# A two-layer hybrid decoder trunk on one core: all weights as one stream that the products feed, and the first block's order

## The chip, the core and the metric

The kernel runs on one core of a Trainium2 chip. The metric is the time of one execution on the device in microseconds (us). Engines are called as the profile calls them: PE is TensorE's matmul and PEld its weight load, DVE is VectorE, ACT is ScalarE, POOL is GpSimd, and SP is the engine whose queue issues nearly all of the DMAs. Every engine takes its own instructions strictly in the order of its list and waits on semaphores for what others produce.

## The reference

The input is one sequence of 512 tokens by 1024 columns in float32; the depth is two layers. Four groups of mixers share one input projection and one output projection, and the residual stream ends in an RMSNorm:

```python
h = x
for l in range(DEPTH):                       # 2 layers
    u = rmsnorm(h, norm_w[l])
    proj = einsum('bsd,de->bse', u, w_in[l])
    ret_p, diff_p, ssd_p, ml_p = split_cols(proj, ...)
    ret_out = retention_mixer(...) * silu(rz)
    diff_out = diff_attention_mixer(...) * silu(dz)
    y = ssd_mixer(...)
    ssd_out = _rms(y * silu(sz)) * ssd_norm_w[l]
    ml_out = mlstm_mixer(...) * silu(mz)
    mix = concatenate([ret_out, diff_out, ssd_out, ml_out])
    h = h + einsum('bse,ed->bsd', mix, w_out[l])
return rmsnorm(h, final_norm_w)
```

The projections are nearly all of the arithmetic. The differential attention takes two softmaxes per head over 512 tokens, and the state-space mixer ("ssd") runs four chunks of 128 tokens with a state carried between them.

## The kernel before

**Arithmetic.** A product in float32 is made of three cheaper ones. An operand x is cut into a high part hi (x rounded by a cast to the type fp32r) and a low part lo = x - hi, and a product is hi·hi + hi·lo + lo·hi, three matmuls that add up in one PSUM bank. For the activations the parts are `uh` and `ul` (lines 347, 348) or `mh` and `ml`, for the weights `whi` and `wlo`.

**Weights.** The input projection has 15 blocks of 512 columns in each layer, the output projection four groups of two halves. A block (or a group) is eight pieces of 128 x 512. `split_w` (lines 364 to 367) brings two pieces with one DMA of 512 KB into a buffer `raw`, of which there are two, and calls `split_half` (lines 351 to 362) for each: ACT writes `whi` (line 357, or 360 where a norm weight is multiplied in), DVE subtracts and writes `wlo` (358 or 361). There are ten buffers each of `whi` and `wlo`, eight in use and two ahead; the cast into a buffer waits until PE has done the last product with the piece that was there. Before the change a block's four DMAs and eight splits are all written where the block's first product is asked for (`load_block`, line 369, called from `proj_tok` and `proj_feat`, and the same in `out_proj`, lines 626 to 635), and the splits stand in a context of priority 100, which makes a scheduler draw them ahead of other work that is written near them.

**Order of the work.** PE's list is a sequence of projections, in the order of `ORDER`: mv, mq, mk, mo, mz, dk, dq, dv, dz, out_proj m, xs, bc, out_proj d, rqk, sz, rv, rz, out_proj s and r. Between the steps of a projection a planner (`drive`, `due`) inserts the steps of the mixers (gates, mlstm, diff, ssd, ret) by an own clock and by the delays in the table `W`. What goes to DVE, ACT, POOL and SP is written in the same pass, and a scheduler orders it by program order and priorities. Buffers and PSUM banks rotate: eight banks, taken from the one that comes free first.

**The first block** (projection mv of layer 0, `start`, lines 373 to 481) is the exception: its order on all engines is written by hand. Token group t (128 tokens, four of them) has squares(t) on ACT, scale(t) (an rsqrt on POOL, line 240), mul(t) (two multiplies on DVE, line 404, tiles `e`), trans(t) (eight transposes on PE, line 131, into two banks, followed by `uh` on ACT and `ul` on DVE); hi(k) and lo(k) split weight piece k. In the strings `orders`, "h3" is the two products with the high part of piece 3 and "l3" the one with its low part. At the very start `warm(4)` and `warm(3)` are matmuls of a tile of ones whose result nobody reads.

**Three other places** that the text below speaks of.

- The differential attention of a head ends with `diff_av` (lines 1148 to 1164): the weights `w` of one token group are transposed into a PSUM bank (line 131) and copied back to SBUF, on DVE for even token groups (line 1157) and on ACT for odd (1155). The bank is then given to the next product that asks for one. On DVE the copy stands in one list with the splits, the sums of the row maxima (1133), the softmax arithmetic (1138 to 1141), `diff_fin` (1177 to 1186) and the gate product `z` (544).
- A chunk of the ssd mixer has a chain on DVE: additions from a broadcast tile `bcm` (line 950), an exponential on ACT and a multiply by a PSUM tile (954), before PE can make the chunk's output (`psacc`, the matmuls that read `w`). The rotary embeddings of the rqk product come in between (`ft`, lines 604 and 606).
- The gates of the mlstm and ssd mixers (`gates`, lines 674 to 802): a scan of small DVE instructions ends in a row that goes to DRAM (`gdr`, line 779) and comes back broadcast to all partitions (`bcm`, line 813).

Of the kernel before, what the change touches and what calls it, by code (L numbers as in the profile page):

```python
# [11 lines left out]
F32 = mybir.dt.float32  # L12
# [11 lines left out]
DEPTH = 2  # L24
# [40 lines left out]
     'm0': 6.4, 's0': 8.8, 'dT1': 0.6, 'dN1': 1.0, 'hp': 100, 'he': 100, 'hr': 50, 'hd': 50, 'dS': 4.7, 'dQ': 6.0,  # L65
# [34 lines left out]
class Trunk:  # L100
    def __init__(self, ctx, tc, aps, dbg=None):
        self.tc, self.nc = tc, tc.nc
        self.x, self.win, self.wg, self.wout, self.nrm, self.rows, self.convp, self.cst, self.out = aps
        self.dbg = dbg or {}
        mk = lambda n, b, **k: ctx.enter_context(tc.tile_pool(name=n, bufs=b, **k))
        self.cp = mk("cp", 1)


        self.small = mk("small", 1)
        self.hp = mk("hp", 1)  # L110
        self.pool = mk("pool", 1)
        self.end = mk("end", 1)
        self.ps = mk("ps", 1, space=bass.MemoryType.PSUM)
        self.banks = [(0.0, b) for b in range(8)]
# [84 lines left out]
    def setup(self):  # L199
# [29 lines left out]
        warm(3)  # L229
# [121 lines left out]
    def split_half(self, raw, scale):  # L351
        nc = self.nc
        hi = self.t("whi", [P, 512], F32R, bufs=10)
        lo = self.t("wlo", [P, 512], F32R, bufs=10)
        with self.tc.high_priority(W["hp"]):
            if scale is None:
                nc.scalar.copy(out=hi, in_=raw)  # L357
                nc.vector.tensor_tensor(out=lo, in0=raw, in1=hi.bitcast(F32), op=ALU.subtract)  # L358
            else:
                nc.scalar.activation(hi, raw, AF.Copy, scale=scale)  # L360
                nc.vector.scalar_tensor_tensor(lo, raw, scale, hi.bitcast(F32), ALU.mult, ALU.subtract)  # L361
        return hi, lo
# [6 lines left out]
    def load_block(self, name):  # L369
        b = BIDX[name]  # L370
        return [q for g in range(4) for q in self.split_w(self.win[self.l, b, :, 2 * g:2 * g + 2, :])]

    def start(self, evac):
# [46 lines left out]
        with self.tc.manual_schedule(engines={E.Activation, E.DVE, E.Pool, E.SP}):  # L420
# [13 lines left out]
            orders = ["h0 h1 l0 l1 h2 h3 h4 h6 l2 h5 l4 l3 h7 l6 l5 l7", "h0 h1 h2 h3 l0 l1 l2 l3 h4 h5 h6 h7 l4 l5 l6 l7"]  # L434
# [16 lines left out]
            lo(4, nc.gpsimd)  # L451
# [4 lines left out]
            mul(1)  # L456
            lo(6, nc.gpsimd)
            lo(3)
            run(pr[0], 6)
            trans(1)  # L460
            lo(5)
            lo(7, nc.gpsimd)
            run(pr[0], 2)
# [12 lines left out]
            self.gates_w()  # L476
            run(pr[2], 8)
# [20 lines left out]
    def proj_tok(self, name, evac, w=None, toks=range(NT), order=None):  # L498
        w = w or self.load_block(name)
        steps = [(t, k, parts) for t in toks for k, parts in order] if order else \  # L500
                [(t, k, (0, 1)) for t, k in self.steps_of(list(toks), name != "mv")]
        banks, n = {}, {}
        for t, k, parts in steps:
# [6 lines left out]
            for part in parts:  # L510
                for u in (self.uh,) if part else (self.uh, self.ul):
                    n[t] += 1
                    self.mm(p, lhsT=u[:, k, ts_], rhs=w[k][part], start=(n[t] == 1), stop=(n[t] == 3 * KD))
# [6 lines left out]
    def proj_feat(self, name, evac):  # L520
        w = self.load_block(name)
        banks = {}
        for f, k in self.steps_of(range(4), True):
            p = banks[f] if k else banks.setdefault(f, self.psum("pj"))
            fs = slice(f * P, (f + 1) * P)
            hi, lo = w[k][0][:, fs], w[k][1][:, fs]
# [100 lines left out]
    def out_proj(self, g, mixt, tok_outer=False, after=None, cut=False, heads=False):  # L627
        nc = self.nc
        gi = GROUPS[g]
        nw = self.nwc[g]  # L630
        w = [[x for q in range(2) for x in self.split_w(self.wout[self.l, gi, half, :, 2 * q:2 * q + 2, :],
                                                        nw[2 * q:2 * q + 2])]
             for half in range(2)]
# [3 lines left out]
        for t, hf in order:  # L637
# [5 lines left out]
            for c0, c1 in zip(cuts, cuts[1:]):  # L643
# [5 lines left out]
                for k in range(4):  # L649
                    hi, lo = w[hf][k]  # L650
# [3 lines left out]
                    self.mm(p, lhsT=mh, rhs=lo[:, cs], start=False, stop=(k == 3))  # L654
                    yield
# [700 lines left out]
```

## Time and profile before

| what | before |
|---|---|
| median of 3 runs | 1045.69 us (1043.56 to 1046.55) |
| profiled execution, its own time | 1043.91 us |
| span from the first to the last instruction | 1042.1 us |
| PE busy | 1023.0 us, 98% of the span |
| DVE busy | 693.2 us, 67% |
| ACT busy | 479.7 us, 46% |
| POOL busy | 164.9 us, 16% |
| mean granted clock of PE | 0.994 of full speed |
| moved by DMA | 93.84 MB |

Times in rows of the profile are us from the start of the span; 1.8 us of the execution's time lie outside it. A row of the timeline gives the start, the time until the end of the group, the engine, the line, the operation and its tiles, and in brackets the idle time before it with what ended it. Matmuls overlap: a row's mean duration is longer than the distance from one to the next. A line of the kernel is written L127; L127 and L131 are the helpers through which every matmul and every transpose goes.

### The profile page before, as it was taken

The numbers are of one execution on the slowest core, as the hardware profiler recorded it, in microseconds if no ns is written. First come the engines' busy times: TensorE is split into PE (matmuls) and PEld (weight loads), VectorE is DVE, ScalarE is ACT, GpSimd is POOL, SyncE is SP. The second block draws the span as 40 slices with busy tenths as digits, with TensorE's granted clock in tenths as the row PEclk, the third lists the DMA queues.
The fourth block names the chain that finished last, engine by engine and source line by source line (L and its number), as shares of the span: only waits on it lengthen the run. The fifth ranks groups of instructions, "written<-read, shape, count | busy, mean of one in ns | idle before, by whom it ended". The sixth has DMA issues, their size and how long they took to land.

```text
span 1042.1 us, 14190 instructions
## 1 busy us (share of the span) xinstructions
PE 1023.0 (98%) x5110; PEld 835.1 (80%) x5110; DVE 693.2 (67%) x1495; ACT 479.7 (46%) x1057; POOL 164.9 (16%) x204
## 2 busy tenths in 40 slices
PE   8999999999999999999999999999999999999997
PEld 6788888877778887878887888887777888878786
DVE  5588675567787867446655967666667786863454
ACT  4444336545455444433343542575444553553332
POOL 2000132101111233022000012210001112510301
PEclk9999999999999999999999999999999999999999
DMA  7324322322212413313122422233121233233112
GB/s 254 107 72 122 102 71 82 101 82 81 79 44 85 128 51 102 102 61 126 41 84 80 138 85 81 82 101 103 60 86 56 81 100 103 81 102 101 42 60 81
DMA packets 39144, 93.84 MB, mean 90 GB/s; under 512 B 3849, under 2 KB 16777, under 8 KB 38946
## 3 DMA queue, kind: packets, MB, share of 16 engines
q1 hardware_dynamic: 38064, 91.49, 28.7%
q10 hardware_dynamic: 1010, 1.45, 0.4%
q8 instruction: 40, 0.66, 0.3%
q14 instruction: 30, 0.25, 0.1%
HBM read 90.78 MB, written 2.15 MB: 89 GB/s over the span
## 4 chain that ended last, share of the span: by engine, by line
PE 90%; DVE 5%; issue 1%; ACT 1%; DMA 1%; POOL 0%; POOLq 0%; DVEq 0%; ACTq 0%
PE pspj L127 74%; PE psS L127 6%; PE psacc L127 6%; PE psS L131 4%; DMA raw<-in_w_in_dram 1%; DVE wlo L361 1%; DVE w L950 1%; DVE ft L606 0%; DVE z L1291 0%; DVE wlo L358 0%; DVE h L657 0%; DVE z L544 0%; ACT e L253 0%; DMA raw<-in_w_out_dram 0%; DVE wlo L418 0%
## 5 line engine op out<-in xcount | busy, mean ns | idle before, releaser
L358 DVE TENSOR_TENSOR wlo<-raw,whi 128x512 fp32r<-128x512 f32 x248 | 174.0, 721 | 67.4 <-ACT whi L357 61.8
L127 PE MATMUL pspj<-whi,uh 128*128 128x512 f32 x512 | 209.7, 410 | 0.0
L127 PE MATMUL pspj<-whi,ul 128*128 128x512 f32 x512 | 200.9, 392 | 0.0
L127 PE MATMUL pspj<-wlo,uh 128*128 128x512 f32 x512 | 197.7, 393 | 2.4 <-DVE wlo L418 2.2
L357 ACT CAST whi<-raw 128x512 fp32r<-128x512 f32 x248 | 147.8, 618 | 108.5 <-PE pspj L127 60.8
L127 PE MATMUL pspj<-uh,whi 128*128 128x512 f32 x448 | 179.2, 400 | 0.0
L127 PE MATMUL pspj<-uh,wlo 128*128 128x512 f32 x448 | 174.7, 390 | 0.0
L127 PE MATMUL pspj<-ul,whi 128*128 128x512 f32 x448 | 174.6, 390 | 0.0
L127 PEld LDWEIGHTS pspj<-wlo,uh 128*128 128x128 f32 x512 | 96.5, 189 | 25.1 <-DVE wlo L418 3.9
L127 PEld LDWEIGHTS pspj<-whi,uh 128*128 128x128 f32 x512 | 97.0, 189 | 22.4 <-issue 3.0
L127 PEld LDWEIGHTS pspj<-whi,ul 128*128 128x128 f32 x512 | 96.9, 189 | 17.8 <-DVE ul L348 0.4
L127 PE MATMUL pspj<-whi,mh 128*128 128x512 f32 (+1 forms) x260 | 105.2, 405 | 4.3 <-DVE w L1157 4.3
L240 POOL TENSOR_TENSOR s<-s,nhalf 128x4 f32<-128x4 f32 (+1 forms) x44 | 35.8, 813 | 417.5 <-DVE s L1181 122.9
L127 PE MATMUL pspj<-whi,ml 128*128 128x512 f32 (+1 forms) x260 | 101.4, 390 | 0.3
L127 PE MATMUL pspj<-wlo,mh 128*128 128x512 f32 (+1 forms) x260 | 101.2, 389 | 0.0
L127 PEld LDWEIGHTS pspj<-uh,wlo 128*128 128x128 f32 x448 | 84.1, 188 | 18.2
L127 PEld LDWEIGHTS pspj<-uh,whi 128*128 128x128 f32 x448 | 84.2, 188 | 17.4 <-issue 0.7
L127 PEld LDWEIGHTS pspj<-ul,whi 128*128 128x128 f32 x448 | 84.3, 188 | 16.0
L584 DVE SCALAR_TENSOR_TENSOR e<-pspj,cvh,e 128x511 f32<-128x511 f32 (+2 forms) x90 | 67.0, 744 | 9.6 <-ACT e L582 8.4
L602 ACT ACTIVATE e<-pspj 32x512 f32<-32x512 f32 x96 | 56.6, 589 | 20.0 <-PE pspj L127 18.7
L657 DVE TENSOR_TENSOR h<-pspj,h 128x512 f32<-128x512 f32 (+1 forms) x65 | 43.6, 678 | 28.7 <-PE pspj L127 28.3
L127 PEld LDWEIGHTS pspj<-whi,mh 128*128 128x128 f32 x260 | 49.3, 190 | 15.4 <-DVE w L1157 5.2
(221 smaller groups left out, 1406.4 us busy)
## 6 DMA issues: line engine op xcount, KB each, us to landing
raw<-in_w_in_dram SPq DMA_DIRECT2D x116, 512.0 KB, 3.9
raw<-in_w_out_dram SPq DMA_DIRECT2D x32, 512.0 KB, 3.5
bcm<-adr SPq DMA_DIRECT2D x16, 256.0 KB, 3.3
z<-in_w_in_dram SPq DMA_DIRECT2D x8, 256.0 KB, 6.6
bcm<-gdr SPq DMA_DIRECT2D x8, 256.0 KB, 3.8
out_dram<-z SPq DMA_DIRECT2D x7, 256.0 KB, 2.0
h<-in_x_dram SPq DMA_DIRECT2D x3, 512.0 KB, 6.5
cst<-in_consts_dram SPq DMA_DIRECT2D x1, 1035.0 KB
```

What stands on the lines that cost most here:

```text
L127: self.nc.tensor.matmul(out, lhsT=lhsT, rhs=rhs, start=start, stop=stop, **kw)
L131: self.nc.tensor.transpose(out, src, self.ident if ident is None else ident)
L240: self.nc.gpsimd.tensor_tensor(out=out, in0=m, in1=self.nhalf[:, :n], op=ALU.pow)
L357: nc.scalar.copy(out=hi, in_=raw)
L358: nc.vector.tensor_tensor(out=lo, in0=raw, in1=hi.bitcast(F32), op=ALU.subtract)
L361: nc.vector.scalar_tensor_tensor(lo, raw, scale, hi.bitcast(F32), ALU.mult, ALU.subtract)
L584: nc.vector.scalar_tensor_tensor(acc[:, s:], p[:, 0:S - s], w[:, 3 - s:4 - s], acc[:, s:], ALU.mult, ALU.add)
L602: nc.scalar.activation(x[q * 32:q * 32 + 32, :], p[o * 32:o * 32 + 32, :], AF.Copy, scale=scale)
L657: nc.vector.tensor_tensor(out=hs, in0=p, in1=hs, op=ALU.add)
L950: nc.vector.scalar_tensor_tensor(e[:, j * P:(j + 1) * P], ab[g][:, j, :], self.ncs[:, t, h:h + 1], self.cap, ALU.add, ALU.min)
```

## The change

**One stream.** A generator `stream` walks through both layers in `ORDER` and yields two pieces at a time, with their DMA and their splits. `feed` draws one such pair from it. `piece(key, k)` returns a piece and feeds until it is there. `proj_tok`, `proj_feat` and `out_proj` take their pieces with `piece` and call `feed` right after the last product with a pair of pieces (the last token or feature group, odd k). So a pair's DMA and splits are now written at the place in the program at which two buffers come free, over the whole kernel, and in particular the first pieces of a block are written before the block itself begins. The splits have no priority any more.

**The first block.** `warm(3)` goes. Token group 0 takes its pieces in the order "h0 h1 l0 l1 h2 h3 h4 h6 l2 h5 h7 l4 l6 l3 l5 l7" and the others take all high parts first. trans(1) stands after h7 of token group 0 and before its l4, l6, l3; lo(4) on POOL stands behind the rsqrt of token group 1; lo(7) goes from POOL to DVE.

```diff
-        with self.tc.high_priority(W["hp"]):
-            if scale is None:
...
+        if scale is None:
+            nc.scalar.copy(out=hi, in_=raw)
+            nc.vector.tensor_tensor(out=lo, in0=raw, in1=hi.bitcast(F32), op=ALU.subtract)
...
-    def load_block(self, name):
-        b = BIDX[name]
-        return [q for g in range(4) for q in self.split_w(self.win[self.l, b, :, 2 * g:2 * g + 2, :])]
+    def stream(self, depth):
+        for l in range(depth):
+            for name in ORDER:
+                if (l, name) == (0, "mv"):
+                    continue
+                if name in BIDX:
+                    for g in range(4):
+                        yield (l, name), self.split_w(self.win[l, BIDX[name], :, 2 * g:2 * g + 2, :])
+                elif name in GROUPS:
+                    for half in range(2):
+                        for q in range(2):
+                            yield (l, name), self.split_w(
+                                self.wout[l, GROUPS[name], half, :, 2 * q:2 * q + 2, :],
+                                self.nwc[name][2 * q:2 * q + 2])
+
+    def feed(self):
+        for key, pieces in self.weights:
+            self.wts.setdefault(key, []).extend(pieces)
+            return
+
+    def piece(self, key, k):
+        while len(self.wts.get(key, ())) <= k:
+            self.feed()
+        return self.wts[key][k]
...
-        warm(3)
...
-            orders = ["h0 h1 l0 l1 h2 h3 h4 h6 l2 h5 l4 l3 h7 l6 l5 l7", "h0 h1 h2 h3 l0 l1 l2 l3 h4 h5 h6 h7 l4 l5 l6 l7"]
+            orders = ["h0 h1 l0 l1 h2 h3 h4 h6 l2 h5 h7 l4 l6 l3 l5 l7", "h0 h1 h2 h3 h4 h5 h6 h7 l0 l1 l2 l3 l4 l5 l6 l7"]
...
-            lo(4, nc.gpsimd)
             scale(1)
             lo(2)
             hi(5)
             hi(7)
             mul(1)
+            run(pr[0], 5)
+            trans(1)
+            lo(4, nc.gpsimd)
             lo(6, nc.gpsimd)
             lo(3)
-            run(pr[0], 6)
-            trans(1)
+            run(pr[1], 4)
             lo(5)
-            lo(7, nc.gpsimd)
-            run(pr[0], 2)
+            lo(7)
+            run(pr[0], 3)
...
             self.gates_w()
+            self.feed()
...
+            if t == NT - 1 and k % 2 and 1 in parts:
+                self.feed()
...
+            if f == 3 and k % 2:
+                self.feed()
...
+                    if t == NT - 1 and k % 2 and c1 % 512 == 0:
+                        self.feed()
```

Lines below 110 keep their numbers; after the change a helper's matmuls are L129 and L133 instead of L127 and L131, and what stood at L540 to L1290 stands 28 to 31 lines further down.

PE's list differs in the first block alone. There, before, the transposes of token group 1 (L131) stand behind the product with the low part of piece 3 (`wlo_214`), and one with a high part (`whi_206`, piece 7) comes after them:

```order
L127 MATMUL pspj_174<-whi_204,uh_75 128x512
L127 MATMUL pspj_174<-whi_204,ul_76 128x512
L127 MATMUL pspj_174<-wlo_194,uh_75 128x512
L127 MATMUL pspj_174<-wlo_214,uh_75 128x512
L131 MATMUL psS_225<-cst,e_208 128x128 x4
L131 MATMUL psS_232<-cst,e_209 128x128 x4
L127 MATMUL pspj_174<-whi_206,uh_75 128x512
L127 MATMUL pspj_174<-whi_206,ul_76 128x512
L127 MATMUL pspj_174<-wlo_212,uh_75 128x512
```

After, at the same place (`whi_199` is piece 5 and `whi_201` piece 7; `pspj_236` belongs to token group 1; `wlo_230`, `wlo_232` and `wlo_234` are the low parts of pieces 4, 6 and 3):

```order
L129 MATMUL pspj_171<-whi_199,uh_75 128x512
L129 MATMUL pspj_171<-whi_199,ul_76 128x512
L129 MATMUL pspj_171<-whi_201,uh_75 128x512
L129 MATMUL pspj_171<-whi_201,ul_76 128x512
L133 MATMUL psS_216<-cst,e_203 128x128 x4
L133 MATMUL psS_223<-cst,e_204 128x128 x4
L129 MATMUL pspj_236<-whi_145,uh_75 128x512
...
L129 MATMUL pspj_171<-wlo_230,uh_75 128x512
L129 MATMUL pspj_171<-wlo_232,uh_75 128x512
L129 MATMUL pspj_171<-wlo_234,uh_75 128x512
```

In both lists 19 products of 512 columns stand between the transposes of token group 0 and those of token group 1; after the change none of the 19 reads the low parts of pieces 3 and 4.

DVE's list in layer 0 ahead of out_proj m, before. `psS_2422` is the bank of one token group of attention transposes, `wlo_2481` to `wlo_2495` are pieces 4 to 7 of out_proj m, `z_2431` and `z_2456` are gate products, `w_2381` is the attention output of the head before:

```order
L1133 TENSOR_REDUCE s_703_2398<-psS_2401 128x1
L361 SCALAR_TENSOR_TENSOR wlo_2481<-raw_2478,cv_131,whi_2480 128x512
L1133 TENSOR_REDUCE s_703_2398<-psS_2402 128x1
L361 SCALAR_TENSOR_TENSOR wlo_2485<-raw_2478,cv_131,whi_2484 128x512
L361 SCALAR_TENSOR_TENSOR wlo_2491<-raw_2488,cv_131,whi_2490 128x512
L361 SCALAR_TENSOR_TENSOR wlo_2495<-raw_2488,cv_131,whi_2494 128x512
L1184 TENSOR_TENSOR s_696_2378<-s_696_2378,s_694_2372 128x4
L544 SCALAR_TENSOR_TENSOR z_2431<-e_2429,pspj_2264 128x512
L1186 TENSOR_TENSOR w_2381<-psacc_2014,s_696_2378 128x512
L544 SCALAR_TENSOR_TENSOR z_2456<-e_2454,pspj_2385 128x512
L1157 COPY w_2424<-psS_2422 128x128
```

After, at the same place (the copy is now `w_2441<-psS_2439`, the four pieces are `wlo_2456`, `wlo_2460`, `wlo_2478` and `wlo_2482`, the gate products `z_2448` and `z_2503`):

```order
L1161 TENSOR_REDUCE s_713_2415<-psS_2419 128x1
L1212 TENSOR_TENSOR s_701_2385<-s_701_2385,s_699_2379 128x4
L361 SCALAR_TENSOR_TENSOR wlo_2456<-raw_2453,cv_128,whi_2455 128x512
L1214 TENSOR_TENSOR w_2388<-psacc_2021,s_701_2385 128x512
L575 SCALAR_TENSOR_TENSOR z_2448<-e_2446,pspj_2271 128x512
L1185 COPY w_2441<-psS_2439 128x128
L1166 RECIPROCAL s_718_2432<-rsum_2282 128x1
L361 SCALAR_TENSOR_TENSOR wlo_2460<-raw_2453,cv_128,whi_2459 128x512
...
L361 SCALAR_TENSOR_TENSOR wlo_2478<-raw_2475,cv_128,whi_2477 128x512
...
L361 SCALAR_TENSOR_TENSOR wlo_2482<-raw_2475,cv_128,whi_2481 128x512
L575 SCALAR_TENSOR_TENSOR z_2503<-e_2501,pspj_2392 128x512
```

Three splits and one gate product that stood ahead of the copy stand behind it. Layer 1 has the same two lists.

DVE's list in layer 0 in the third chunk of the ssd mixer, before: `ft_3787` is a rotary embedding, `wlo_3902` and `wlo_3906` are two pieces of one DMA, `w_3838` is the chunk's tile that L954 multiplies:

```order
L604 SCALAR_TENSOR_TENSOR ft_3787<-pspj_3668,cst 128x512
L358 TENSOR_TENSOR wlo_3896<-raw_3889,whi_3895 128x512
L358 TENSOR_TENSOR wlo_3902<-raw_3899,whi_3901 128x512
L358 TENSOR_TENSOR wlo_3906<-raw_3899,whi_3905 128x512
L606 TENSOR_TENSOR ft_3787<-ft_3787,e_3782 128x512
L978 TENSOR_TENSOR w_3812<-psacc_3809,g_144_575 128x512
L992 TENSOR_TENSOR state_3818<-psS_3815,state_3818 128x512
L950 SCALAR_TENSOR_TENSOR w_3838<-bcm_3822,g_148_583,cap 128x128 x2
```

After (`ft_3804`, `wlo_3830` and `wlo_3834`, `w_3875`):

```order
L635 SCALAR_TENSOR_TENSOR ft_3804<-pspj_3675,cst 128x512
L358 TENSOR_TENSOR wlo_3818<-raw_3811,whi_3817 128x512
L637 TENSOR_TENSOR ft_3804<-ft_3804,e_3799 128x512
L358 TENSOR_TENSOR wlo_3830<-raw_3827,whi_3829 128x512
L358 TENSOR_TENSOR wlo_3834<-raw_3827,whi_3833 128x512
L1006 TENSOR_TENSOR w_3849<-psacc_3846,g_149_582 128x512
L1020 TENSOR_TENSOR state_3855<-psS_3852,state_3855 128x512
L978 SCALAR_TENSOR_TENSOR w_3875<-bcm_3859,g_153_590,cap 128x128 x2
```

The addition to `ft` stands ahead of the two splits instead of behind them; the rest of the row is the same, in both layers.

More of the change, by code (lines that the diff above doesn't have):

```diff
@@ L64 @@
      'sN': 0.0, 'sF': 7.3, 'rC': 2.3, 'rN': 3.0, 'dT': 9.14, 'dN': 1.0, 'dM': 3.0, 'dV': 6.68, 'dF': 14.0,
-     'm0': 6.4, 's0': 8.8, 'dT1': 0.6, 'dN1': 1.0, 'hp': 100, 'he': 100, 'hr': 50, 'hd': 50, 'dS': 4.7, 'dQ': 6.0,
+     'm0': 6.4, 's0': 8.8, 'dT1': 0.6, 'dN1': 1.0, 'he': 100, 'hr': 50, 'hd': 50, 'dS': 4.7, 'dQ': 6.0,
      'ha': 50}
@@ L113, in __init__ @@
         self.ps = mk("ps", 1, space=bass.MemoryType.PSUM)
+        self.weights = self.stream(DEPTH)
+        self.wts = {}
         self.banks = [(0.0, b) for b in range(8)]
@@ L354, in split_half @@
         lo = self.t("wlo", [P, 512], F32R, bufs=10)
-        with self.tc.high_priority(W["hp"]):
-            if scale is None:
[L357 to L361, printed above, removed]
+        if scale is None:
+            nc.scalar.copy(out=hi, in_=raw)
+            nc.vector.tensor_tensor(out=lo, in0=raw, in1=hi.bitcast(F32), op=ALU.subtract)
+        else:
+            nc.scalar.activation(hi, raw, AF.Copy, scale=scale)
+            nc.vector.scalar_tensor_tensor(lo, raw, scale, hi.bitcast(F32), ALU.mult, ALU.subtract)
         return hi, lo
@@ L498, in proj_tok @@
     def proj_tok(self, name, evac, w=None, toks=range(NT), order=None):
-        w = w or self.load_block(name)
+        toks = list(toks)
+        key = self.l, name
+        get = (lambda k: w[k]) if w else (lambda k: self.piece(key, k))
         steps = [(t, k, parts) for t in toks for k, parts in order] if order else \
-                [(t, k, (0, 1)) for t, k in self.steps_of(list(toks), name != "mv")]
+                [(t, k, (0, 1)) for t, k in self.steps_of(toks, name != "mv")]
         banks, n = {}, {}
@@ L512, in proj_tok @@
                     n[t] += 1
-                    self.mm(p, lhsT=u[:, k, ts_], rhs=w[k][part], start=(n[t] == 1), stop=(n[t] == 3 * KD))
+                    self.mm(p, lhsT=u[:, k, ts_], rhs=get(k)[part], start=(n[t] == 1), stop=(n[t] == 3 * KD))
+            if t == NT - 1 and k % 2 and 1 in parts:
+                self.feed()
             yield
@@ L520, in proj_feat @@
     def proj_feat(self, name, evac):
-        w = self.load_block(name)
+        key = self.l, name
         banks = {}
@@ L525, in proj_feat @@
             fs = slice(f * P, (f + 1) * P)
-            hi, lo = w[k][0][:, fs], w[k][1][:, fs]
+            hi, lo = [x[:, fs] for x in self.piece(key, k)]
             self.mm(p, lhsT=hi, rhs=self.uh[:, k, :], start=(k == 0), stop=False)
@@ L628, in out_proj @@
         nc = self.nc
[L629 to L633, printed above, removed]
         l = self.l
@@ L649, in out_proj @@
                 for k in range(4):
-                    hi, lo = w[hf][k]
+                    hi, lo = self.piece((l, g), 4 * hf + k)
                     mh, ml = m(t, k)
```

## The prediction

> **What bounds the kernel now.** I read the page's span and busy times first.
>
> ```profile
> span 1042.1 us, 14190 instructions
> PE 1023.0 (98%) x5110; PEld 835.1 (80%) x5110; DVE 693.2 (67%) x1495; ACT 479.7 (46%) x1057; POOL 164.9 (16%) x204
> ```
>
> PE is busy for all but 19.1 us of the span, and the change leaves it the same products (only the three `warm` ones go). So nothing can be won but idle time of PE and time in which PE is slow. Where that lies shows the table of windows of 20 us (columns: length, busy times of PE, PEld, DVE, ACT, POOL, granted clock, DMA share, GB/s):
>
> ```profile
> 0.00:20.00 20.00, 16.57 (x50) 10.72 (x51) 10.27 (x21) 7.72 (x16) 5.65 (x10) 0.96 0.85 305
> 60.00:80.00 20.00, 20.00 (x92) 16.54 (x91) 19.45 (x44) 10.27 (x20) 0.00 (x0) 1.00 0.40 112
> 240.00:260.00 20.00, 17.87 (x88) 13.89 (x88) 14.82 (x32) 11.30 (x29) 2.72 (x5) 1.00 0.32 105
> 400.00:420.00 20.00, 18.52 (x94) 15.36 (x93) 15.36 (x32) 9.18 (x18) 3.93 (x5) 1.00 0.26 80
> 740.00:760.00 20.00, 17.80 (x95) 13.12 (x94) 15.94 (x45) 12.31 (x36) 2.40 (x5) 0.98 0.23 64
> 760.00:780.00 20.00, 20.00 (x107) 15.94 (x106) 12.20 (x30) 6.32 (x20) 0.31 (x1) 0.93 0.21 69
> 900.00:920.00 20.00, 18.40 (x87) 15.32 (x86) 16.48 (x28) 9.28 (x17) 6.53 (x6) 0.91 0.43 132
> 1020.00:1040.00 20.00, 14.81 (x77) 12.58 (x75) 10.77 (x24) 5.25 (x15) 3.49 (x5) 0.98 0.26 102
> ```
>
> Of the idle time 3.43 us lie at the start, 2.13 + 2.20 at 240 and 740 (the same place in the two layers), 1.48 + 1.60 at 400 and 900, and 5.19 (plus the last 2) in the tail, whose list the change leaves alone. In layer 1 the clock falls behind both places: 0.02 x 20 + 0.07 x 20 = 1.8 us of full-speed work lost after 740, and 0.09 x 20 = 1.8 after 900. The waits of PE name the causes (us in total, times, longest):
>
> ```profile
> PE pspj L127 <- DVE w L1157: 4.3, 2, 2.2
> PE psacc L127 <- DVE w L954: 3.1, 2, 1.6
> PE pspj L127 <- DVE wlo L418: 2.2, 1, 2.2
> PE psacc L127 <- DVE w L846: 0.7, 2, 0.3
> ```
>
> The first three are places whose order the change turns; at the fourth it doesn't, so those 0.7 us stay.
>
> **The start.** These rows are the start of the timeline, with one steady stretch of 512-column products and one split that no other engine disturbs:
>
> ```profile
> 6.15 1.47 DVE L404 SCALAR_TENSOR_TENSOR e<-h,s,psS 128x512 f32<-128x512 f32 x2 [0.67 <-POOL s L240]
> 6.76 1.65 PE L127 MATMUL psS<-ones 128*128 128x128 f32 x6
> 8.20 1.92 PE L131 MATMUL psS<-cst,e 128*128 128x128 f32 x8
> 13.08 1.42 POOL L418 TENSOR_TENSOR wlo<-z,whi 128x512 fp32r<-128x512 f32 x1 [6.96 <-DVE whi L414]
> 14.45 1.01 POOL L240 TENSOR_TENSOR s<-s,nhalf 128x1 f32<-128x1 f32 x1
> 15.43 2.49 POOL L418 TENSOR_TENSOR wlo<-z,whi 128x512 fp32r<-128x512 f32 x2
> 15.49 1.40 DVE L404 SCALAR_TENSOR_TENSOR e<-h,s,psS 128x512 f32<-128x512 f32 x2 [0.45 <-POOL s L240]
> 16.82 1.66 DVE L418 TENSOR_TENSOR wlo<-z,whi 128x512 fp32r<-128x512 f32 x1
> 18.53 0.80 PE L127 MATMUL pspj<-wlo,uh 128*128 128x512 f32 x1 [2.24 <-DVE wlo L418]
> 19.12 1.91 PE L131 MATMUL psS<-cst,e 128*128 128x128 f32 x8
> 20.22 0.59 ACT L347 CAST uh<-psS 128x512 fp32r<-128x512 f32 x1 [5.65 <-PE psS L131]
> 22.30 0.68 DVE L418 TENSOR_TENSOR wlo<-z,whi 128x512 fp32r<-128x512 f32 x1
> 161.81 44.93 PE pspj L127 x198
> ```
>
> The first of the two `e` is there at 6.15 + 1.47 / 2 = 6.9, but the eight transposes start at 8.20, behind `warm(3)`. Without it they start 1.3 us earlier. Later PE waits 2.24 us for l3, which DVE makes at 16.82 behind mul(1), and mul(1) waits for an rsqrt that starts at 14.45 because lo(4) is ahead of it on POOL. After the change the rsqrt can start at about 13.8, mul(1) is done at about 15.7 instead of 16.9, and the transposes of token group 1 no longer wait for l3. Before, they end at 19.12 + 1.91 = 21.03. The same 19 products stand ahead of them in both lists. Bounded below, they start at 15.7 and at full speed take 1.1 (estimate from 512 columns in 44.93 / 198 = 0.227, and the eight here, which at half speed take 1.91): 16.8. Bounded above, they start at 16.3 and take 1.91: 18.2. What they feed comes next now (h0 of group 1 with no other product between), and the cast `uh` that it reads ended 20.22 + 0.59 - 19.12 = 1.7 us after the first transpose, beside h7's products; now PE waits for it and for `ul`, some 0.85 us (my estimate, 1.7 and one more DVE row of 0.7 less the transposes' 1.1 and the first products' 0.5). So the gain lies between 21.03 - 18.2 - 0.85 = 2.0 and 21.03 - 16.8 + 0.4 = 4.6; I take **3.8**, near the upper end, because every row on DVE's side moves forward by 1.2 and the wait of 2.24 has nothing left to come from.
>
> The eight transposes at 8.20 took 1.92, as long as the eight at 19.12: both ran at half clock, so `warm` had bought nothing by 8.20 and the clock comes full somewhat later. The Trainium skill (TensorE: Matmul & The Clock Gate, "What's actually happening") says that the array is throttled by default and runs full only after a window of about 3.4 us in which it was busy, the windows running freely. By that rule taking `warm` out of a start with gaps can cost one more such window, about 1.7 us by its figure; this speaks against the change and is weighed as a rival below.
>
> **The copy ahead of out_proj m.** In layer 0, where PE waits 2.13, and the same products of layer 1 in the chain:
>
> ```profile
> 246.65 0.38 PE L131 MATMUL psS<-cst,w 128*128 128x128 f32 x2
> 246.89 2.24 DVE L361 SCALAR_TENSOR_TENSOR wlo<-raw,cv,whi 128x512 fp32r<-128x512 f32 x3
> 250.31 0.68 DVE L544 SCALAR_TENSOR_TENSOR z<-e,pspj 128x512 f32<-128x512 f32 x1
> 250.91 0.29 DVE L1157 COPY w<-psS 128x128 f32<-128x128 f32 x1
> 251.25 0.50 PE L127 MATMUL pspj<-whi,mh 128*128 128x512 f32 x1 [2.13 <-DVE w L1157]
> 251.25 2.35 PE pspj L127 x9
> 759.33 3.86 PE pspj L127 x9
> ```
>
> The transposes were done at 247.03, and the copy that empties their bank came at 250.91, because three splits (2.24) and a `z` (0.68) stood ahead of it. They now stand behind: 251.20 - 2.9 = 248.3 for its end. Other small rows change places, and two splits that used to be earlier fall into this stretch, against one `qs` that leaves it; played through row by row the copy ends between 248.2 and 248.8. PE arrives at 251.25 - 2.13 = 249.1. So the wait goes, with 0.3 to 0.9 to spare: 2.13 + 2.20 = 4.3 us. The nine products behind it take 3.86 in layer 1 against 2.35 in layer 0, 1.5 us of half clock; with the 1.8 of the windows I take 1.6 for it. Next late is nothing: the three splits belong to the second half of out_proj m, which PE reaches after the 48 products of the first, 48 x 0.227 = 10.9 us later. Together **5.9**; the lower bound, if the copy comes 1.3 late, is half the wait without the clock: 2.0.
>
> **The ssd chunk.** DVE around the second place:
>
> ```profile
> 394.36 1.29 DVE L358 TENSOR_TENSOR wlo<-raw,whi 128x512 fp32r<-128x512 f32 x2 [1.72 <-ACT whi L357]
> 395.57 1.56 DVE L606 TENSOR_TENSOR ft<-ft,e 128x512 f32<-128x512 f32 x1
> 397.05 0.68 DVE L978 TENSOR_TENSOR w<-psacc,g 128x512 f32<-128x512 f32 x1
> 404.11 1.27 DVE L954 TENSOR_TENSOR w<-w,psS 128x512 f32<-128x512 f32 x2
> ```
>
> DVE waits 1.72 for the two splits' data with the `ft` addition behind them, and then runs without a gap up to the multiply at 404.11 for which PE waits. The addition now fills the wait, so the row behind it starts 397.05 - 395.57 = 1.48 earlier, and so does the multiply, unless the data come later or the `ft` input is not there yet. Of the waits of 1.5 and 1.6 about 1.3 each goes, and with them layer 1's half clock, 1.6 to 1.8: 2.6 + 1.6 = **4.2**, bounds 1.3 and 4.9. The addition took 1.56 instead of the 0.68 of the row at 397.05, with the same size of tile. The Trainium skill (GPSIMD Engine Reference, "8. Key points") says that POOL shares its ports to SBUF with VectorE and gets in the way of DVE instructions with two inputs in SBUF; the split of 1.66 at 16.82, beside POOL's 15.43 to 17.92, against 0.68 at 22.30 agrees. By that rule the addition in its new place, if POOL works there, still takes 1.56, nearly all of the gap of 1.72.
>
> **Everything else.** The splits lose their priority in all 37 blocks of the stream (29 of the input projection and 8 groups of the output projection). What holds them is shown by two rows of the page, the cast's and the broadcast's:
>
> ```profile
> L357 ACT CAST whi<-raw 128x512 fp32r<-128x512 f32 x248 | 147.8, 618 | 108.5 <-PE pspj L127 60.8
> bcm<-gdr SPq DMA_DIRECT2D x8, 256.0 KB, 3.8
> ```
>
> Most of ACT's idle ahead of a cast ends with PE giving back a buffer: the weights are early by the ring of ten, and a split may move by some instructions before PE sees it. The one place where DVE has no slack is 60 to 80, with 19.45 of 20 us busy, and its like in layer 1. There the gates' scan and a tile that waits for `bcm` (3.8 us from issue to landing) now stand ahead of late pieces; I find 0.2 to 0.3 us to spare, so 0 to 0.8 a layer, I take **-0.4** for both. All other places 0 (bounds -1 and +0.5, the waits at 337 and 847).
>
> **The sum.** 3.8 + 5.9 + 4.2 - 0.4 = 13.5, against the profiled execution 1043.91 - 13.5 = 1030.4. The median of the three runs, 1045.69, lies 1.8 above it; I put the forecast 1.1 higher, at **1031.5**. The best ends give 4.6 + 6.1 + 4.9 + 0.5 = 16.1: 1027.8; the worst 2.0 + 2.0 + 1.3 - 1.6 - 1 = 2.7: 1041 to 1043.
>
> **The rivals.**
>
> Half of it: the copy and the multiply stay late by 1 us each, because DVE's rows there run beside POOL at 1.3 to 1.66 instead of 0.68. Each wait of about 1 costs 4 us over both places and layers, and one of 1.5 us sufficed at 900 to lose the clock for 1.8; with two such dips 4 + 3.5 = 7.5 of the 13.5 are lost: 1039. For it: the row at 395.57. Against: the copy has 0.3 to 0.9 to spare, and POOL is busy for 2.7 of 20 us there.
>
> The clock at the start: without `warm` one window of half speed more, 1.7 us: 1033. For it: the half-clock transposes at 8.20. Against: the transposes move up by what is taken out, so that PE is as dense as before.
>
> The stream does nothing: ring and buffers `raw` set the times of the splits as before, and only the first block gains, 1045.7 - 3.8 = 1042. Against: DVE's list itself has the copy ahead of three splits.
>
> Slower: without priority the low part of a pair reaches DVE behind the mixers' work in every block, and PE runs up against it. One wait per block of 13.5 / 37 = 0.36 us eats the whole gain; above that the kernel is slower, and at 0.7, one DVE row's length, 37 x 0.7 = 26 makes it 1031.5 + 26 = 1057. For it: DVE at 19.45 of 20. Against: PE's waits for splits are 2.2 us in all before, and DVE is only 67% busy.
>
> **How the numbers follow.** Forecast, with its bounds: 0.60. Clock at the start: 0.12. Half: 0.14. Stream does nothing: 0.04. Slower: 0.10. A measurement of this kernel tells about 0.3%, 3.1 us, from no change, so 1042.6 and below is faster. The range reaches from 1026, the best end with 1.8 for the spread of the runs, to 1042: it leaves out the slower rival and the outer ends of the others. Half and the idle stream reach over the bound with 0.05: faster 0.85, same 0.06, slower 0.09.
>
> **What would show it.** Right: no wait on the copy (L1157 before) and at most 0.4 on the multiply (L954 before) in the waits of PE; granted clock 1.00 in the windows after 730 and 890; transposes of token group 1 ending before 18; PE's idle down from 19.1 to about 10. Wrong: waits of PE on `wlo` of lines 358 or 361 in several blocks, or a dip of the clock in a window that had none.

## The result, and the profile after

The changed kernel takes 1033.09 us (median of 4 runs, 1032.04 to 1034.02), the kernel before 1044.62 (4 runs, 1039.93 to 1046.55): a ratio of 0.9896, 95% interval 0.9874 to 0.9917. In the comparisons of the experiments the kernel before ran many more times, with medians of 1042.89 (19 runs) to 1044.87 (8), so its three runs that were shown first lay high, and the change is worth 10 to 11 us. The forecast was 1031.5. One run of a later experiment, of 1445.86 us at a mean granted clock of 0.655, is left out of that experiment's time and ratio.

The page's span and busy times after, and the waits of PE (helpers and late lines have moved: L129, L133, L982 and L1041 were L127, L131, L954 and L1013):

```profile
span 1032.2 us, 14180 instructions
PE 1019.2 (99%) x5104; PEld 830.1 (80%) x5104; DVE 691.7 (67%) x1496; ACT 479.8 (46%) x1057; POOL 161.8 (16%) x203
```
```profile
PE psS L133 <- ACT w L1041: 1.6, 2, 1.0
PE psacc L129 <- DVE w L982: 1.5, 2, 0.8
PE psacc L129 <- DVE w L874: 0.6, 2, 0.3
PE psS L129 <- DVE ft L620: 0.5, 1, 0.5
```

The wait on the copy (4.3 us before) is gone from the list, the one on the first block's split (2.2 before) is down to 0.2, the one on the ssd multiply is halved, and two lines are new: one on the ssd mixer's last activation (L1041) and one on a convolution's output (L620). The windows of the same stretches of time:

```profile
0.00:20.00 20.00, 18.38 (x56) 11.16 (x57) 10.79 (x25) 10.43 (x22) 4.22 (x9) 1.00 0.88 311
240.00:260.00 20.00, 20.00 (x107) 15.57 (x106) 15.70 (x39) 10.43 (x29) 3.15 (x5) 1.00 0.36 106
740.00:760.00 20.00, 20.00 (x103) 15.67 (x102) 17.15 (x41) 12.00 (x33) 3.15 (x5) 1.00 0.25 79
900.00:920.00 20.00, 19.27 (x96) 16.05 (x95) 15.04 (x30) 10.13 (x19) 4.04 (x5) 1.00 0.20 61
920.00:940.00 20.00, 18.98 (x90) 15.42 (x89) 8.16 (x16) 8.79 (x17) 1.10 (x2) 1.00 0.33 102
```

PE is full at 240 and 740, the granted clock is 1.00 in all five (0.96, 0.98 and 0.91 before in the first, third and fourth), and idle time is left at 900, in part new at 920. Behind the first block PE has the same list in both kernels, so from the second row on the start of one and the same product can be compared; the first row compares the place from which 32 products of the first block are left. This gives the account by place:

| product (start in the span, us) | before | after | earlier by |
|---|---|---|---|
| the last 32 products of the first block | 33.39 | 30.46 | 2.9 |
| behind the convolution's output at 95 | 97.93 | 95.95 | 2.0 |
| first of out_proj m, layer 0 | 251.25 | 246.97 | 4.3 |
| the ssd chunk's output, layer 0 | 404.93 | 399.92 | 5.0 |
| transposes of the ssd output, layer 0 | 429.56 | 425.31 | 4.3 |
| first of out_proj m, layer 1 | 759.33 | 752.77 | 6.6 |
| 7 products on, at the end of the half clock before | 762.48 | 754.37 | 8.1 |
| the ssd chunk's output, layer 1 | 914.63 | 905.65 | 9.0 |
| 23 products on, the same there | 919.68 | 909.07 | 10.6 |
| transposes of the ssd output, layer 1 | 940.89 | 931.42 | 9.5 |
| end of the span | 1042.1 | 1032.2 | 9.9 |

### The profile page after: what moved, and what is told of

The parts are those of the page before. It is cut to its first block, busy times and chain, and to the rows that moved or that the text cites. A ratio compares the mean times of both kernels' runs of the same rounds, so it can differ in the third digit from the quotient of the medians.

```text
span 1032.2 us, 14180 instructions
## 1 busy us (share of the span) xinstructions
PE 1019.2 (99%) x5104; PEld 830.1 (80%) x5104; DVE 691.7 (67%) x1496; ACT 479.8 (46%) x1057; POOL 161.8 (16%) x203
## 4 chain that ended last, share of the span: by engine, by line
PE 87%; DVE 6%; DMA 3%; issue 2%; ACT 2%; SPq 0%; POOL 0%; POOLq 0%; DVEq 0%; ACTq 0%
PE pspj L129 72%; PE psacc L129 6%; PE psS L129 6%; PE psS L133 4%; DMA raw<-in_w_in_dram 2%; DVE wlo L358 1%; DVE w L978 1%; DMA z<-in_w_in_dram 1%; DVE wlo L361 0%; DVE z L1319 0%; DVE h L685 0%; DVE z L575 0%; DVE e L615 0%; ACT e L254 0%; SPq L449 0%
## 5 line engine op out<-in xcount | busy, mean ns | idle before, releaser
L358 DVE TENSOR_TENSOR wlo<-raw,whi 128x512 fp32r<-128x512 f32 x248 | 171.7, 715 | 64.2 <-ACT whi L357 60.0
L129 PE MATMUL pspj<-whi,uh 128*128 128x512 f32 x512 | 209.3, 409 | 0.1
L357 ACT CAST whi<-raw 128x512 fp32r<-128x512 f32 x248 | 147.8, 619 | 117.9 <-PE pspj L129 58.7
L129 PE MATMUL pspj<-whi,ul 128*128 128x512 f32 x512 | 200.9, 392 | 0.2 <-DVE ul L349 0.2
L129 PE MATMUL pspj<-wlo,uh 128*128 128x512 f32 x512 | 196.7, 392 | 0.2 <-DVE wlo L441 0.2
L129 PE MATMUL pspj<-uh,whi 128*128 128x512 f32 x448 | 179.2, 400 | 0.0
L129 PE MATMUL pspj<-uh,wlo 128*128 128x512 f32 x448 | 174.9, 390 | 0.0
L129 PE MATMUL pspj<-ul,whi 128*128 128x512 f32 x448 | 174.7, 390 | 0.0
L129 PEld LDWEIGHTS pspj<-whi,uh 128*128 128x128 f32 x512 | 96.7, 189 | 22.9 <-issue 3.0
L129 PEld LDWEIGHTS pspj<-wlo,uh 128*128 128x128 f32 x512 | 96.2, 188 | 22.3 <-DVE wlo L441 1.3
L129 PEld LDWEIGHTS pspj<-whi,ul 128*128 128x128 f32 x512 | 96.8, 189 | 18.7 <-DVE ul L349 1.4
L129 PE MATMUL pspj<-whi,mh 128*128 128x512 f32 (+1 forms) x260 | 104.3, 401 | 0.0
L129 PE MATMUL pspj<-whi,ml 128*128 128x512 f32 (+1 forms) x260 | 100.9, 388 | 0.3 <-DVE ml L654 0.2
L129 PE MATMUL pspj<-wlo,mh 128*128 128x512 f32 (+1 forms) x260 | 100.7, 387 | 0.0
L129 PEld LDWEIGHTS pspj<-uh,wlo 128*128 128x128 f32 x448 | 84.1, 188 | 18.5 <-DVE wlo L358 0.5
L129 PEld LDWEIGHTS pspj<-uh,whi 128*128 128x128 f32 x448 | 84.2, 188 | 17.3 <-issue 0.7
L129 PEld LDWEIGHTS pspj<-ul,whi 128*128 128x128 f32 x448 | 84.3, 188 | 16.0
L1162 ACT ACTIVATE w<-psS,s 128x128 f32<-128x128 f32 (+3 forms) x64 | 33.2, 523 | 56.0 <-DVE s L1161 55.8
```

Of the source, the lines that this page charges most:

```text
L129: self.nc.tensor.matmul(out, lhsT=lhsT, rhs=rhs, start=start, stop=stop, **kw)
L1162: nc.scalar.activation(pe[j][:, 0:n], s[:, 0:n], AF.Exp, bias=nm[:, j:j + 1], accum_out=r[:, t, j:j + 1])
```

## The experiments

**One part at a time.** First the new first block alone:

```diff
 # the kernel before, with warm(3) removed and start() as after the change (without its feed)
-            orders = ["h0 h1 l0 l1 h2 h3 h4 h6 l2 h5 l4 l3 h7 l6 l5 l7", ...
+            orders = ["h0 h1 l0 l1 h2 h3 h4 h6 l2 h5 h7 l4 l6 l3 l5 l7", ...
```

> The kernel before with the new first block alone (order of the pieces, trans(1) earlier, the rsqrt ahead of lo(4), no warm(3)); weights as before. My theory: PE is 2.9 us earlier at 33 us, as in the trace of the whole change, 2.0 to 2.9 us earlier from there on, and the waits on the copy (4.3), the ssd multiply (3.1) and their clock dips stay: time 1041.5, ratio 0.997. Rival: the rest of the kernel gives the start's gain back, since DVE between 60 and 100 us is full: PE no earlier than before behind 100 us, ratio 1.000.

It takes 1042.39 (10 runs) against 1042.89 (19 runs), ratio 0.9985, interval 0.9972 to 0.9998. In its trace PE is 2.6 us earlier at the first product of mq (38.06 against 40.65) and still 2.5 earlier at out_proj m (248.72 against 251.25). But the clock then dips elsewhere, and of these 2.5 us the median shows only 0.5. Windows of this kernel, to be set against those of before in the prediction:

```profile
240.00:260.00 20.00, 17.94 (x81) 13.75 (x79) 13.22 (x28) 8.97 (x22) 2.71 (x5) 0.91 0.32 105
400.00:420.00 20.00, 18.53 (x86) 15.19 (x85) 14.16 (x31) 9.21 (x18) 3.02 (x4) 0.91 0.25 75
740.00:760.00 20.00, 17.95 (x97) 13.24 (x95) 15.37 (x43) 11.91 (x36) 1.81 (x3) 1.00 0.20 63
900.00:920.00 20.00, 18.60 (x95) 15.62 (x95) 16.67 (x29) 9.47 (x18) 6.84 (x7) 1.00 0.41 131
```

The waits are the same four as before, 1.4 to 2.1 us each, but the half clock now follows both of layer 0 (0.91 at 240 and at 400) and the first of layer 1 (0.66 from 760 to 765), where in the run of before it followed both of layer 1 (0.91 at 900, and 1.00 here) and none of layer 0. So it differs between runs which of the four waits is followed by a dip, and the scatter of the kernel before fits this: its fastest run, 1039.9, had a mean granted clock of 0.998 and its slowest, 1047.5, one of 0.991, which is some 7 us of 1042 (an estimate); the changed kernel, with 0.999 in all four runs and no dip ahead of the tail in its trace, stays within 2 us. My theory holds for the position of PE, and the rival (all given back by 100 us) falls.

Then the stream alone, with the old first block:

```diff
 # the changed kernel, with warm(3) and start() as before the change (and its feed)
```

> The changed kernel with the old first block (and warm(3)): the stream alone. My theory: the copy's wait gone (4.3), the ssd multiply's wait halved (1.5 of 3.1), two clock dips gone in layer 1 (3.2), a new wait of 1.6 to 1.9 behind the ssd's last activation: 6.5 to 8 us less than before, ratio 0.993. With the old start the conv wait at 95 us (0.7) should not appear, since PE comes there 2 us later. Rival: the stream gains because of the earlier start of the weights after the first block, and without it gains under 3 us, ratio over 0.997.

1036.03, ratio 0.9919 (0.9895 to 0.9943); waits of 1.8 on the multiply and 1.4 on the last activation, none on the convolution. As expected. So far the stream seemed to carry the gain.

**Is it the stream, or the priority?** The change does two things to the splits: it writes them elsewhere, and it takes their priority. Taking the priority from the output projection's splits alone, with no stream:

```diff
-        with self.tc.high_priority(W["hp"]):
+        with self.tc.high_priority(W["hp"] if scale is None else 1):
```

> The kernel before with the priority taken from the splits of the output projection alone (lines 360 and 361); the priority of all other splits and the place at which all are issued stay. On DVE the copy ahead of out_proj m then stands where it stands after the change. My theory: what mattered there is the drop of the priority and not the stream: the wait on the copy (4.3 us) and layer 1's clock dip behind it (1.6) go, nothing else changes: 5.9 us less, ratio 0.994. Rival: the stream is needed, because pieces and buffers come as late as before: wait of 2 us a layer on the copy or on a split of out_proj m, ratio 1.000.

1035.53, ratio 0.9916 (0.9894 to 0.9938): as much as the whole stream, and 1.5 us more than I expected; in its trace the half clock behind the multiply of layer 1 did not come either (1.00 from 900 to 1020, 0.66 from 915 to 920 before), which my theory had not said. Of the waits of PE behind the first 2 us this is left, beside the 0.7 that stays everywhere:

```profile
PE psacc L127 <- DVE w L954: 3.1, 2, 1.6
PE pspj L127 <- DVE wlo L418: 2.2, 1, 2.2
```

The copy's wait has gone entirely, and DVE's rows show why (timeline of this kernel): one split, `w` and `z`, then the copy, with the other splits behind.

```profile
246.01 0.75 DVE L361 SCALAR_TENSOR_TENSOR wlo<-raw,cv,whi 128x512 fp32r<-128x512 f32 x1
246.67 0.69 DVE L1186 TENSOR_TENSOR w<-psacc,s 128x512 f32<-128x512 f32 x1
247.27 0.68 DVE L544 SCALAR_TENSOR_TENSOR z<-e,pspj 128x512 f32<-128x512 f32 x1
247.86 0.29 DVE L1157 COPY w<-psS 128x128 f32<-128x128 f32 x1
```

It ends at 248.15 where it ended at 251.20 before. The rival, that the stream was needed for it, falls. The same test on the whole change, giving the priority back:

```diff
+        with self.tc.high_priority(100):
+            if scale is None:
...
```

> The changed kernel with the splits' priority of 100 given back: stream and new first block stay. DVE's list then has the copy behind four splits again and the ft addition behind its two, as before the change. My theory: the drop of the priority did the work at both places, not the stream: the waits on the copy (about 4.2 us in all) and on the ssd multiply (about 3) come back, with clock dips of 1.6 at one or two of the four places, and the time is that of the kernel with the new first block alone, 1042, ratio 0.999. Rival: the stream brings the pieces early enough for the splits to stand in front without harm, and most of the gain stays: under 1036.

1050.65, ratio 1.0064 (1.0044 to 1.0084): slower than the kernel before, and 8.3 us slower than the new first block alone. The direction of my theory holds, but it had 1042: beside the old waits there are two new ones.

```profile
PE psacc L129 <- DVE w L983: 5.1, 4, 1.7
PE pspj L129 <- DVE w L1186: 4.1, 2, 2.1
PE psS L133 <- DVE w L803: 2.9, 2, 1.5
```

The multiply (L983) now holds PE up four times instead of twice, and the gates' scan (L803) once in each layer. And the other way round, the kernel before with the priority taken from all splits and nothing else:

```diff
-        with self.tc.high_priority(W["hp"]):
-            if scale is None:
+        if scale is None:
...
```

> The kernel before with the splits' priority taken away and nothing else: blocks are issued where they were, the first block is the old one. My theory: the copy and the ft addition stand ahead as after the change, so it gains what the stream with the old first block gained: waits on the copy gone, on the multiply about 1.6 in all, 1035 to 1036, ratio 0.993. Rival: without the stream, splits without priority come late, because a block's eight are written behind other work: waits of PE on wlo in several blocks, ratio over 1.000.

1031.99, ratio 0.9889 (0.9872 to 0.9905): with the old first block and no stream at all this is 4.0 us faster than the stream with the old first block. Its waits, beside the 1.0 ahead of the first product that every run has, are

```profile
PE pspj L127 <- DVE wlo L417: 2.2, 1, 2.2
PE psacc L127 <- DVE w L845: 0.6, 2, 0.3
```

No wait on the copy, on the multiply, or on a split outside the first block. My theory said 1035 to 1036 and was too low on the gain; the rival, splits that come late, falls outright.

**The rotary addition by itself.**

```diff
-            nc.vector.tensor_tensor(out=r, in0=r, in1=x, op=ALU.add)
+            with self.tc.high_priority(60): nc.vector.tensor_tensor(out=r, in0=r, in1=x, op=ALU.add)
```

> The kernel before with nothing changed but the addition of the rotary embedding (line 606) given a priority of 60, which moves four instructions of DVE ahead of two splits each, two in each layer, in the ssd stretch. My theory: the addition fills DVE's wait for a DMA, the multiply's wait (L954) falls from 1.6 to about 0.8 a layer, as after the whole change, and layer 1's dip of the clock (1.6) goes: 3 us less, ratio 0.997. Rival: the multiply waits for the weights' DMA by way of something else and stays at 1.5 a layer, ratio 1.000.

1041.15 (10 runs), ratio 0.9971 (0.9958 to 0.9985). The multiply's wait falls from 3.1 to 1.4, as after the change, so the place of four additions is the cause of that half. The medians differ by 1.7 us, not by the 3 expected, since the dips do not go with the wait: in the profiled run, which took 1044.24, the clock dipped at 250, 405 to 415 and 760, the second of them behind the multiply of layer 0, whose wait was only 0.78.

**The three parts without the stream.**

```diff
 # new first block; no priority for the output projection's splits; priority 60 for the rotary addition
```

> The three parts without the stream: the kernel before with the new first block, no priority for the splits of the output projection alone, and a priority of 60 for the rotary addition. My theory: start 2.4 to 2.9, copy 4.3, multiply 1.6, and none of the waits that came new with the whole change (1.6 to 1.9 behind the ssd's last activation, 0.7 at the conv): span about 1031, time 1031 to 1033, no slower than the whole change (1033.1). Rival: the stream has a part of its own in the gain, and this stays 2 us or more behind it.

1032.64, ratio 0.9893 (0.9872 to 0.9913): no slower than the whole change, as expected. The three named places are the gain, and the stream is not needed for any.

**The clock at the start.**

```diff
             self.mm(self.nw[half], lhsT=self.ones[0:1, :], rhs=row[:, half * 512:(half + 1) * 512])
+        warm(3)
```

> The changed kernel with warm(3) put back. My theory: the transposes of token group 0 start 1.3 us later again, and as the second group's wait for mul(1), which hangs on DMA, ACT, DVE and POOL alone, hardly anything of it is left behind the second transposes: 0 to 1.3 us slower, ratio 1.000 to 1.001 against the changed kernel (1033 to 1034.5). Rival, the clock: with warm(3) the full clock comes one window of 3.4 us earlier, and the kernel is up to 1.7 us faster, 1031.5.

1033.26, ratio 0.9901 (0.9885 to 0.9918), against 1033.09 without: no difference that these runs can tell. The clock rival falls; so does the notion that `warm(3)` cost anything once the second token group waits for its own chain.

**What the stream costs, and how far a split can wait.** Without the stream, without priority and with the new first block:

```diff
 # the kernel before, with start() as after the change, no warm(3), and split_half without its priority
```

> The kernel before with the splits' priority taken away and the new first block, without the stream. My theory: the two parts add up: the span of the kernel without priority, 1030.1, less what the new start gives against a start with its clock dip, 2.0 to 2.9: 1027.5 to 1028.5, time 1029.5 to 1030.5, 2.5 to 3.5 faster than the whole change, so that the stream by itself costs time. Rival: the new start is eaten behind 60 us by a DVE that is full, or waits on wlo appear: 1032, the same as without the new start.

1029.28, ratio 0.9868 (0.9851 to 0.9884): the first block's 2.7 us add to the 1031.99, and the stream costs 3.8. Then the stream with its feeds written later:

```diff
-                self.feed()
+                self.later(3.0, self.feed)
 # at all three places of the products; also 5.0 and 10.0
```

> The changed kernel with each feed written 3.0 us later by the planner's clock, so the splits stand later in the lists; everything else as after the change. My theory: what costs in the stream is that its pairs are written too early, ahead of the mixers' work; 3 us later DVE's list in the ssd stretch is that of the kernel without priority, the waits on the multiply (1.5) and behind the ssd's last activation (1.6) go, 2.5 to 3.5 us less than the whole change: 1030. Rival: those waits come of the one DMA queue or the buffers and not of the place in the list: 1033, the same.

> The same with 5.0 us. My theory: a second step on the same scale: no further gain, 1030, if the ring of ten buffers still covers it; if not, the first waits of PE on wlo or whi of line 357 to 361 appear, up to 5 us in all: 1030 to 1035. Rival as for 3.0 us: 1033, the same, with the ssd waits still there.

> The changed kernel with each feed written 10 us later by the planner's clock, beside 3.0 and 5.0 us. My theory: somewhere on this scale the weights come late. At 3.0 and 5.0 PE waited once for a split, 1.3 and 0.4 us; at 10 us, over 40 products later, nearly all pairs are written only when a product asks for them, several blocks wait for whi or wlo, 0.4 us each in some 10 blocks or more: 1033 to 1040, slower than with 5.0 us. Rival: the scheduler puts the splits by their readiness and not by where they are written, so a further delay changes nothing: 1029 to 1030, waits on wlo under 1.5 in all.

With 3.0 us: 1029.47 to 1031.18 (three runs), ratio 0.9874 (0.9854 to 0.9895). With 5.0: 1029.48, ratio 0.987 (0.9851 to 0.9889). With 10: 1039.0, ratio 0.9943 (0.9922 to 0.9963). At 3.0 and at 5.0 the waits of the ssd stretch have gone; at 3.0 PE waits once for a split, 1.3 us at 520, and at 5.0 only 0.4:

```profile
PE psacc L129 <- DVE w L874: 0.7, 2, 0.3
PE pspj L129 <- DVE ul L349: 0.4, 2, 0.2
PE pspj L129 <- DVE wlo L358: 0.4, 1, 0.4
```

At 10 the copy's wait is back:

```profile
PE pspj L129 <- DVE w L1185: 2.8, 2, 2.1
PE pspj L129 <- DVE wlo L358: 2.1, 1, 2.1
PE psacc L129 <- DVE w L982: 1.7, 1, 1.7
```

The time at 10 us is what I expected, the cause only in part: there is one wait on a split, not ten. What comes back is the old kind of wait. As I read its list, that is because pairs that are written too late come in a bunch again when a product asks for them: in DVE's list three splits then stand ahead of the copy where there was one at 3.0.

One row shows the two ends: how long DVE stood idle with a split at the head of its list, waiting for the cast (L357 before, from the groups of lines; here of the stream with the priority, and of the kernel before without it).

```profile
L359 DVE TENSOR_TENSOR wlo<-raw,whi 128x512 fp32r<-128x512 f32 x248 | 176.9, 736 | 73.2 <-ACT whi L358 67.8 <-PE pspj L129 3.9 <-PE psS L133 0.9
```
```profile
L357 DVE TENSOR_TENSOR wlo<-raw,whi 128x512 fp32r<-128x512 f32 x248 | 174.2, 719 | 57.2 <-ACT whi L356 52.4 <-PE pspj L127 3.6 <-PE psS L131 0.8
```

67.8 us for the slowest kernel, 61.8 for the kernel before, 60.0 for the changed one, 52.4 without priority. The work is the same 248 subtractions. But the row does not order all kernels: e_sc has 62.8, more than the kernel before, and is 7.4 us faster; e_stream has 55.8, less than the changed kernel, and is 2.9 us slower. What counts is whether work for which PE soon waits stands behind such a split, and that is read at the place and not from the total.

## Why the prediction was right, and where its steps were off

The time lies in the range and 1.6 us above the forecast, which is closer than the sum was. The sum was 13.5 from the profiled run before, and the two profiled runs lie 9.9 apart (1043.91 and 1034.02). Of the 3.6 missing, 1.1 is hidden by the allowance for the high first median, and 0.9 because the profiled run after was the slowest of its four; that part of the agreement is luck. Of the signs that were named, three came: no wait on the copy, a granted clock of 1.00 after 730 and 890, and the second transposes done before 18. Two did not: the wait on the multiply is 1.5, not at most 0.4, and PE is idle for 13.0, not about 10. Step by step, against the account by place:

**The start**: 3.8 forecast, bounds 2.0 and 4.6, measured 2.9 at 33 us. The mechanism is as told. Rows of the timeline after:

```profile
6.79 1.99 PE L133 MATMUL psS<-cst,e 128*128 128x128 f32 x8
15.31 1.41 DVE L427 SCALAR_TENSOR_TENSOR e<-h,s,psS 128x512 f32<-128x512 f32 x2 [0.45 <-POOL s L241]
16.19 1.24 PE L133 MATMUL psS<-cst,e 128*128 128x128 f32 x8
17.47 0.50 PE L129 MATMUL pspj<-whi,uh 128*128 128x512 f32 x1
```

The first transposes start at 6.79 (forecast 6.9), mul(1) ends at 16.7 instead of 15.7, because the rsqrt started at 14.35 instead of 13.8 and lasted 0.93 where the forecast leaves it 0.5, and the second transposes end at 17.43 at full clock. The rsqrt's moving past lo(4) was thus worth 0.1 (14.45 to 14.35), not 0.7: the DVE rows that feed it came late too. The half clock behind the wait of 2.24 (0.85 from 15 to 20, 0.80 from 20 to 25) cost 1.7 us before and nothing after, where it is 1.00; the sum counted it for the transposes alone (1.91 against 1.1). The clock's coming full later without `warm(3)` was read rightly, but is small: the first product of 0.40 starts at 12.79, against one of 0.39 at 11.82 before. The granted clock shows 1.00 there in both kernels, so this is read from the lengths: a product of 0.79 at 9.94 before is as long as the one of 0.80 at 18.53, where the granted clock falls to half. On the half clock behind waits the trace agrees with the Trainium skill (TensorE: Matmul & The Clock Gate, "What's actually happening") in the length of the dips, about 3.4 us (0.78, 0.50, 0.50 and 0.52 in the four us from 18), but not with idle time of a whole window as what it takes: waits of 0.8 to 2.2 us were enough, sometimes.

**The copy**: 5.9 forecast, measured 2.3 and 2.3 for the waits and 1.6 for layer 1's clock, 6.2. The copy starts at 245.74 and PE reaches out_proj m at 246.97, so it had 0.9 to spare, as played through. That the place in DVE's list decides is shown by e_sc, and by e_hp, where four splits stand ahead of it again and the wait is 4.1.

**The ssd chunk**: 4.2 forecast, bounds 1.3 and 4.9, measured 0.7, 0.9 and 1.6, 3.2. The sign and place are right, the gain at each of the two waits was forecast as 1.3. DVE's rows after:

```profile
390.10 1.29 DVE L358 TENSOR_TENSOR wlo<-raw,whi 128x512 fp32r<-128x512 f32 x2 [1.16 <-ACT whi L357]
391.31 0.68 DVE L1006 TENSOR_TENSOR w<-psacc,g 128x512 f32<-128x512 f32 x1
395.29 2.69 DVE L978 SCALAR_TENSOR_TENSOR w<-bcm,g,cap 128x128 f32<-128x128 f32 x6
399.11 1.27 DVE L982 TENSOR_TENSOR w<-w,psS 128x512 f32<-128x512 f32 x2
```

The row behind the splits starts 1.2 after them, where it started 2.7 after them before: the 1.48 were won. But the six additions from `bcm` took 2.69 instead of 2.09, beside POOL's work on the rotary embedding at 395.42, and the multiply starts 9.0 behind the splits against 9.75 before. My bound of the mechanism named POOL for the addition only, not for the rows that moved next to it; the addition itself took 0.68 in its new place, at 388.26, where POOL does nothing. That POOL is the cause of those 0.6 us is read from the overlap, not tried.

**Everything else**: 0 with bounds of -1 and +0.5, and 0.4 lost in the gates' stretch. This is the step that failed: it cost 3, and not where the 0.4 was looked for (PE is busy for 20.00 of 20 from 60 to 80). At 95 us a convolution's output came 0.7 late (1.0 with what was lost on the way there, 0.1 in layer 1), and the ssd mixer's last activation cost 0.75 and 1.1. The rows of the latter:

```profile
420.04 1.29 DVE L358 TENSOR_TENSOR wlo<-raw,whi 128x512 fp32r<-128x512 f32 x2 [0.40 <-ACT whi L357]
421.25 0.68 DVE L575 SCALAR_TENSOR_TENSOR z<-e,pspj 128x512 f32<-128x512 f32 x1
424.53 0.72 ACT L1041 ACTIVATE w<-w,s 128x512 f32<-128x512 f32 x1 [0.57 <-DVE s L1040]
425.31 0.66 PE L133 MATMUL psS<-cst,w 128*128 128x128 f32 x4 [0.60 <-ACT w L1041]
```

DVE waits for the cast of a pair with the gate product `z` behind it; `z` starts the chain to the activation for which PE waits. A pair that the stream writes ahead of `z` thus does there what the priority did at the copy. I had looked for weights that come late and found slack everywhere; what came late was the mixers' work behind weights that were early. e_nohp and the feeds written 3.0 and 5.0 us later have no such wait.

**The rivals.** "Half of it" came closest in kind, since the multiply stayed late by 0.8 each, but no clock dip followed. "The stream does nothing" was right about the stream and wrong about the time: I had not separated the stream from the dropped priority, which is a change of its own and the larger one. The slower rival had the sign of the effect wrong: without priority the splits stand later, and later by 3 or 5 us was better again. The clock at the start came late by 1 us, as said above, and cost nothing that shows in the time (e_warm).

## What to carry to other kernels

A load or split that feeds the bottleneck engine need not stand first in a helper engine's list: what counts is that it is there in time, and every row that it passes while its own data are not there makes the others wait. Where a ring of buffers gives slack, place such work as late as the ring allows, and where the bottleneck waits, look for that work at the head of the helper's list with its data not there. And when an edit does two things, the place and the priority here, run each alone before giving the credit to the larger one: the old kernel without its priority gave 1031.99, the rewritten stream with the old start 1036.03. The fastest of all, 1029.28, has no stream, and the stream fed 5 us later, 1029.48, is no faster.

## What the runs showed that was not expected

The granted clock falls to half for about 3.4 us after idle times of PE of only 0.8 to 2.2 us, but not each time: the four waits of the kernel before were followed by a dip in layer 1 alone in its trace (0.73 from 760 to 765, 0.66 from 915 to 920), in layer 0 twice and in layer 1 once with the new first block. In e_sc, with PE idle 1.5 and 1.6 us at 400 and 900, there was none. The shortest that sufficed were 0.78 in e_ft and 0.82 in v_nost, both ahead of the ssd chunk's output of layer 0. In v_nost:

```profile
PE psacc L127 <- DVE w L954: 1.7, 2, 0.8
395.00:400.00 5.00, 4.18 (x22) 3.24 (x21) 5.00 (x11) 2.48 (x5) 0.84 (x1) 1.00 0.28 80
400.00:405.00 5.00, 4.97 (x20) 4.09 (x20) 2.90 (x8) 1.44 (x3) 0.96 (x2) 0.66 0.41 132
```

The changed kernel waits 0.78 at the same product (399.92) and keeps 1.00. What decides is not shown by these runs. Each dip of the account by place costs 1.5 to 1.6 us, so a short wait of PE can cost twice what the table of waits shows, and one of 0.8 three times. Dips also go with the scatter of a kernel's time: 7.6 us over all runs of the kernel before, under 1.3 over four runs each for v_best and e_later50, which have no such wait behind the start.
